# The last layer norm of a decoder trunk: the mean of the second half of the tokens from row sums of the weights

## The chip, the cores and the metric

The kernel runs on one core of one Trainium2 chip, as one launch. The metric is the device time in microseconds (us) of one execution. The kernel before took 795.58 us, the median of 3 runs (795.56 to 795.65).

## The reference, cut to what matters

256 tokens of width 2048 pass two layers (a pooling layer and a block-sparse attention layer, each with a memory branch). Only the end of the second layer is touched here: the output projection, the residual sum and the layer norm, all in fp32.

```
y = mixed @ w_out[i]                                  # (256, 2048) @ (2048, 2048)
h = layer_norm(DEEPNORM_ALPHA * h + y, ln_g[i], ln_b[i])

def layer_norm(x, g, b):
    mu = x.mean(-1, keepdims=True)
    var = jnp.square(x - mu).mean(-1, keepdims=True)
    return (x - mu) * lax.rsqrt(var + LN_EPS) * g + b
```

The output is this last h. Its norm needs, for each token, a mean and a variance over all 2048 columns.

## The kernel before, in words

**Precision.** Every fp32 operand of a product is split into a high and a low part (`split`, L72 to L75: ScalarE copies the high part, VectorE subtracts to get the low one), and each product is made of three matmuls: high by high, high by low, low by high.

**Blocks.** Weights come in blocks of 1024 columns a partition (512 KB). The list `items` holds them in the order in which TensorE uses them, and `run` (L174 to L212) walks it: loads are issued on SyncE (SP) some items ahead, each block is split (`prep`) three items ahead, and TensorE's matmuls of an item take 12 instructions. A block lands in one of four `raw` buffers, and its load waits until the split of the block four before has read that buffer; some blocks land in `ebuf`, `p` or `gate` instead (`SPOT`, L839). Each engine takes its instructions in the order in which the code writes them.

**The last projection.** `out_proj(1, range(3))` gives 24 items for the columns 0 to 1535. Its eight blocks for the last 512 columns (`KEEP`, L838 to L852) are loaded and split on the way, but not multiplied: both parts stay in `kept`, two planes of 16 x 512 columns in the tile `xm`. After `run`, TensorE works from `kept` alone (`last`, L879 to L889): for each of the 16 row blocks k three matmuls, so 48 for one accumulator. The tokens are two halves of 128, t = 0 and t = 1.

**The end of the kernel before.** TensorE does t = 0 over all 512 columns, then t = 1 over columns 1536 to 1791, then t = 1 over 1792 to 2047 (this last accumulator is `end`; two matmuls by an identity, the `seed`, add the residual to it). While these run, VectorE makes the norm of t = 0 and prepares t = 1: a preliminary mean m0 of the first 1536 columns is subtracted, the result is multiplied by g and split once more (`times_g`, L916). When `end` is there, its statistics give the true mean and deviation; TensorE then adds, to each piece of t = 1, the preliminary product by the identity and a product of six rows ("factor products": the two numbers of each token, transposed, times rows of g and b that `load_gb_rows` and `split_rows` made earlier, L820 to L836). What comes out of PSUM is scaled by the reciprocal deviation by ScalarE and VectorE and stored (L987 to L1002).

Of the kernel before, what the change touches and what calls it, by code (L numbers as in the profile page):

```python
# [11 lines left out]
F32 = mybir.dt.float32  # L12
# [37 lines left out]
def trunk(ctx: ExitStack, tc: tile.TileContext, a: dict, out: bass.AP):  # L50
# [6 lines left out]


    KX = KT * 2 * T
    near = sb.tile([P, 96], F32, name="near")  # L60
    xm = sb.tile([P, 2 * KX], F32R, name="xm")
    xT, memT = kept = [xm[:, i * KX:(i + 1) * KX].rearrange("p (k t) -> p k t", k=KT) for i in range(2)]
    zT = sb.tile([P, KT, 2 * T], F32R, name="zT")
    res = U0 = U1 = S0 = S1 = ident = mask = psc = eps_t = stats = ebuf = gate = None

# [58 lines left out]
    def prep_piece(it, c0, c1):  # L124
        raw = it["raw"][:, c0:c1]
        kind, *to = it["dst"] or ("w",)
        if kind == "act":
            t, kb = to
            k0, k1 = 4 * kb + c0 // T, 4 * kb + c1 // T
            split(t[:, k0:k1, :T], t[:, k0:k1, T:], raw.rearrange("p (k t) -> p k t", t=T))  # L130
            return
        if "w" not in it:
            it["w"] = to or (sb.tile([P, BLK], F32R, name="wh", bufs=W_BUFS),
                             sb.tile([P, BLK], F32R, name="wl", bufs=W_BUFS))
        wh, wl = it["w"]
# [682 lines left out]
    gbt = {}

    def load_gb_rows():  # L820
        raw = heads_tile("qq").rearrange("p a b -> p (a b)")[:6]
        gbt["rows"] = heads_tile("kk").rearrange("p a b -> p (a b)")[:6]
        gbt["hi"] = val_tile().rearrange("p a b c -> p (a b c)")[:6]
        gbt["sel"] = sb.tile([6, 2], F32, name="sel")
        for nm, p0 in (("ln_g", 0), ("ln_b", 3)):
            nc.scalar.dma_start(gbt["sel"][p0:p0 + 3], a["sel"][:3])
            nc.scalar.dma_start(f(raw)[p0:p0 + 3], a[nm][1][None, :].to_broadcast([3, D]))
        for n in range(4):
            later(31 + n, lambda n=n: split_rows(f(raw)[:, n * 512:(n + 1) * 512], n))

    def split_rows(raw, n):
        hi, rows = (gbt[k][:, n * 512:(n + 1) * 512] for k in ("hi", "rows"))
        nc.scalar.activation(hi, raw, AF.Copy)
        nc.vector.tensor_scalar_mul(f(hi), f(hi), gbt["sel"][:, 0:1])
        nc.vector.scalar_tensor_tensor(rows, raw, gbt["sel"][:, 1:2], f(hi),
                                       op0=ALU.mult, op1=ALU.add)  # L836

    KEEP = (9, 11, 13, 15, 17, 19, 21, 23)  # L838
    SPOT = {2: 0, 3: 1, 4: 2, 5: 0, 6: 1, 7: 2}  # L839
# [2 lines left out]
             lambda: gate[:, :4].rearrange("p a t -> p (a t)"))  # L842
    for j, it in enumerate(out_proj(1, range(3))):
        items.append(it)
        if j == 0:
            after(load_gb_rows)
        if j in KEEP:
            kb = KEEP.index(j)
            w3 = [t[:, 2 * kb:2 * kb + 2].rearrange("p k n -> p (k n)") for t in kept]
            item(a["w_out"][1, 3, kb], BLK, None, ("keep", *w3))  # L850
            if kb in SPOT:
                items[-1].update(lead=5 if kb == 2 else FAR, spot=spots[SPOT[kb]])  # L852

# [36 lines left out]

    def add(t, c0, c1, o):
        r = res[:, t, 1536 + c0:1536 + c1]
        nc.vector.scalar_tensor_tensor(r, r, ALPHA, o, op0=ALU.mult, op1=ALU.add)
        nc.vector.bn_stats(stats[:, t, 3 + (c0 > 0)], r)

    def finish(t, *chunks):
        for n in chunks:
            norm_chunk(n, t, gb1[n])
            for c0 in (n * 512, n * 512 + 256):
                store(t, c0, c0 + 256)  # L900

    cc = sb.tile([P, 6], F32R, name="cc").rearrange("p (v c) -> p v c", v=2)
    m0 = sb.tile([P, 2], F32, name="m0")
    ds = sb.tile([P, 2], F32, name="ds")
# [5 lines left out]
    place_of = {1: (0, 0), 0: (0, 512), 2: (1, 0), 3: (1, 512)}  # L910

    def both(n, c0, c1):
        i, at = place_of[n]
        return [t[:, at + c0:at + c1] for t in parts[i]]

    def times_g(n, c0=0, c1=512):  # L916
        r = res[:, 1, n * 512 + c0:n * 512 + c1]
        nc.vector.scalar_tensor_tensor(r, r, m0[:, 0:1], gb1[n][0][:, c0:c1],
                                       op0=ALU.subtract, op1=ALU.mult)
        hi, lo = both(n, c0, c1)  # L920
        nc.scalar.activation(hi, r, AF.Copy)
        return lambda: nc.vector.tensor_sub(lo, r, f(hi))

    def store(t, c0, c1, src=None, by=None):
        (by or nc.sync).dma_start(out[t * P:(t + 1) * P, c0:c1], res[:, t, c0:c1] if src is None else src)

    o = last(0, 0, 512)
    nc.vector.bn_aggr(m0, stats[:, 1, :3].rearrange("p a b -> p (a b)"))
    r = res[:, 1, 1792:]
    seed = both(3, 256, 512)  # L930
    nc.scalar.activation(seed[0], r, AF.Copy, scale=ALPHA)
    for low in [times_g(1), times_g(2), times_g(0, 256, 512)]:
        low()
    nc.vector.scalar_tensor_tensor(seed[1], r, ALPHA, f(seed[0]), op0=ALU.mult, op1=ALU.subtract)
    add(0, 0, 512, o)
    norm_stats(0, 4)
    o = last(1, 0, 256)
    finish(0, 0, 1)
    add(1, 0, 256, o)
    low = times_g(3, 0, 256)  # L940
    finish(0, 2)
    low()
    finish(0, 3)
    end = last(1, 256, 512, seed)


    pieces = (1, 0, 256), (1, 256, 512), (2, 0, 512), (0, 256, 512), (3, 0, 256)
    ts = {at: ps.tile([P, 512], F32, name="acc", bufs=4)[:, :at[2] - at[1]] for at in pieces[2:]}
    ts[pieces[0]] = ps.tile([P, 512], F32, name="o")[:, :256]
    ts[pieces[1]] = ps.tile([P, 2, 512], F32, name="s2")[:, 0, :256]  # L950
    for at in pieces:
        hi, lo = both(*at)
        mm(ts[at], one, hi, True, False)
        mm(ts[at], one, lo, False, False)
    nc.vector.bn_stats(stats[:, 1, 4], end)  # L955


    mv = sb.tile([P, 2], F32, name="mv", bufs=2)
    nc.vector.bn_aggr(mv, stats[:, 1].rearrange("p a b -> p (a b)"))  # L959
    rs = sb.tile([P, 1], F32, name="rs", bufs=2)  # L960

    def centred(n, c0, c1, src=None):
        r = res[:, 1, n * 512 + c0:n * 512 + c1]
        nc.vector.scalar_tensor_tensor(r, r if src is None else src, mv[:, 0:1], gb1[n][0][:, c0:c1], op0=ALU.subtract, op1=ALU.mult)  # L964

    def scaled(n, c0, c1):
        r = res[:, 1, n * 512 + c0:n * 512 + c1]
        nc.vector.scalar_tensor_tensor(r, r, rs, gb1[n][1][:, c0:c1], op0=ALU.mult, op1=ALU.add)
        store(1, n * 512 + c0, n * 512 + c1)

    nc.scalar.activation(ds[:, 1:2], mv[:, 1:2], AF.Sqrt, bias=eps_t[:, 0:1])
    nc.vector.tensor_sub(ds[:, 0:1], m0[:, 0:1], mv[:, 0:1])
    nc.scalar.activation(cc[:, :, 0:3:2], ds[:, :, None].to_broadcast([P, 2, 2]), AF.Copy)
    centred(3, 256, 512, end)
    nc.vector.tensor_sub(cc[:, :, 1], ds, f(cc[:, :, 0]))  # L975
    pt = ps.tile([P, 512], F32, name="pt")[:6, :P]
    nc.tensor.transpose(pt, f(cc).rearrange("p v c -> p (v c)"), ident)  # L977
    cct = sb.tile([P, P], F32R, name="ident")[:6]
    nc.scalar.activation(cct, pt, AF.Copy)  # L979
    for n, c0, c1 in pieces:  # L980
        mm(ts[n, c0, c1], cct, gbt["rows"][:, n * 512 + c0:n * 512 + c1], False, True)
    nc.vector.reciprocal(rs, ds[:, 1:2])
    scaled(3, 256, 512)
    centred(0, 0, 256)
    scaled(0, 0, 256)
    e = ebuf.rearrange("p j c -> p (j c)")

    def emptied(n, c0, c1):
        nc.scalar.activation(e[:, (n - 1) * 512 + c0:(n - 1) * 512 + c1], ts[n, c0, c1], AF.Copy, scale=rs)  # L989

    def sent(n, c0, c1, by):
        store(1, n * 512 + c0, n * 512 + c1, e[:, (n - 1) * 512 + c0:(n - 1) * 512 + c1], by)

    for at in pieces[:3]:
        emptied(*at)
    sent(*pieces[0], nc.sync)
    sent(*pieces[1], nc.scalar)
    for n, c0, c1 in pieces[3:]:
        r = res[:, 1, n * 512 + c0:n * 512 + c1]
        nc.vector.tensor_scalar_mul(r, ts[n, c0, c1], rs)  # L1000
        store(1, n * 512 + c0, n * 512 + c1)
    sent(*pieces[2], nc.scalar)  # L1002
# [55 lines left out]
```

## Time and profile before

| | |
|---|---|
| median of the runs | 795.58 us |
| the profiled execution | 795.69 us |
| its span, first to last instruction | 793.9 us |
| TensorE's granted clock, mean of the span | 0.997 |
| share of the chain that ended last | TensorE 98% |
| from the last product of `end` (785.86) to the end of the span | 8.0 us |

In the profile PE is TensorE, PEld its weight loads, DVE is VectorE, ACT is ScalarE, SP is SyncE; SPq and ACTq are the two queues on which DMAs are issued. Times are us from the start of the span; L70 is line 70 of the kernel. A row of the timeline gives start, busy time, engine, line, operation, out<-in, shapes and count, and in brackets how long the engine sat idle before it and for whom. Rows of grouped instructions give the busy time of all, the mean of one in ns, and the idle time before them.

### The profile page before, as it was taken

The page shows a single profiled execution, that of the slowest core. Times are in us where ns is not written, and L with a number is a line of the kernel's source. Part 1 is how long each engine was busy: PE and PEld are TensorE (multiplying, and loading weights), DVE is VectorE, ACT ScalarE, POOL GpSimd, SP SyncE. Part 2 cuts the span into 40 slices and gives each one's busy share as a digit, 9 for nine tenths or more (in the row PEclk, how much of TensorE's full clock was granted, in tenths as well). Part 3 has the DMA queues.
Part 4 walks back from the last instruction along what each step waited for, and adds up shares of the span by engine and source line. Part 5 has one row for each costly group of instructions (what it writes and reads, how often), then busy time and mean ns, then how long its engine had stood idle before and what let it go on. Part 6 is the DMA issues. An engine that isn't in the chain of part 4 may idle for free.

```text
span 793.9 us, 10030 instructions
## 1 busy us (share of the span) xinstructions
PE 787.4 (99%) x3664; PEld 657.3 (83%) x3664; DVE 574.3 (72%) x778; ACT 483.6 (61%) x595; POOL 0.2 (0%) x4
## 2 busy tenths in 40 slices
PE   9999999999999999999999999999999999999997
PEld 6888888888888888888888888888888888888886
DVE  6764588867488665668658786996578856878966
ACT  5666657576666543489865866566756566565531
POOL 0000000000000000000000000000000000000000
PEclk9999999999999999999999999999999999999998
DMA  9977566787768865599885685558764677747923
GB/s 338 404 239 168 188 187 185 214 243 213 216 233 214 293 206 190 188 287 264 247 239 160 193 229 194 179 174 223 240 185 163 196 214 226 210 163 260 332 70 106
DMA packets 121769, 172.16 MB, mean 217 GB/s; under 512 B 58226, under 2 KB 61042, under 8 KB 121458
## 3 DMA queue, kind: packets, MB, share of 16 engines
q1 hardware_dynamic: 119968, 167.41, 69.4%
q10 hardware_dynamic: 1752, 4.12, 1.5%
q8 instruction: 28, 0.46, 0.2%
q14 instruction: 21, 0.17, 0.1%
HBM read 156.29 MB, written 2.10 MB: 200 GB/s over the span
## 4 chain that ended last, share of the span: by engine, by line
PE 98%; DMA 1%; ACT 0%; DVE 0%; ACTq 0%; issue 0%
PE acc L70 91%; PE s L70 3%; PE o L70 3%; PE pt L70 2%; DMA raw<-in_w_mk 1%; ACT ebuf L989 0%; ACTq L113 0%; DVE stats L955 0%; DVE wh L159 0%; ACT L180 0%; DVE res L964 0%; DVE mv L959 0%; PE pt L977 0%; ACT ident L979 0%; DVE cc L975 0%
## 5 line engine op out<-in xcount | busy, mean ns | idle before, releaser
L75 DVE TENSOR_TENSOR wl<-raw,wh 128x1024 fp32r<-128x1024 f32 x234 | 279.3, 1206 | 137.7 <-ACT wh L74 133.7
L70 PE MATMUL acc<-wh,xm 128*128 128x512 f32 x1408 | 352.0, 390 | 0.2 <-DVE wh L159 0.2
L74 ACT ACTIVATE wh<-raw 128x1024 fp32r<-128x1024 f32 x234 | 239.1, 1041 | 139.3 <-PE acc L70 72.7
L70 PEld LDWEIGHTS acc<-wh,xm 128*128 128x128 f32 x1408 | 263.1, 188 | 54.4 <-ACT wh L158 0.6
L70 PE MATMUL acc<-wl,xm 128*128 128x512 f32 x704 | 191.7, 389 | 0.0
L70 PEld LDWEIGHTS acc<-wl,xm 128*128 128x128 f32 x704 | 132.2, 188 | 27.4
L70 PE MATMUL acc<-wh,zT 128*128 128x512 f32 x448 | 112.0, 390 | 0.0
L70 PEld LDWEIGHTS acc<-wh,zT 128*128 128x128 f32 x448 | 83.7, 188 | 17.1
L70 PE MATMUL acc<-xm 128*128 128x512 f32 x288 | 66.3, 389 | 0.0
L391 DVE STREAM_TRANSPOSE p<-ebuf 32x192 f32<-32x192 f32 (+1 forms) x160 | 63.3, 396 | 2.4
L70 PEld LDWEIGHTS acc<-xm 128*128 128x128 f32 x288 | 53.7, 188 | 10.9
L70 PE MATMUL acc<-wl,zT 128*128 128x512 f32 x224 | 61.0, 389 | 0.0
L70 PEld LDWEIGHTS acc<-wl,zT 128*128 128x128 f32 x224 | 42.1, 188 | 8.7
L75 DVE TENSOR_TENSOR xm<-raw,xm 128x1024 fp32r<-128x1024 f32 (+2 forms) x31 | 36.2, 1180 | 10.2 <-ACT xm L74 10.0
L74 ACT ACTIVATE xm<-raw 128x1024 fp32r<-128x1024 f32 (+2 forms) x31 | 30.5, 1015 | 6.1 <-PE acc L70 3.0
L290 ACT ACTIVATE pl<-acc 128x1024 uint16<-128x1024 uint16 x26 | 26.2, 1025 | 8.0 <-PE acc L70 8.0
L74 ACT ACTIVATE pp<-p 128x384 fp32r<-128x384 f32 (+1 forms) x20 | 11.2, 559 | 32.3 <-DVE p L391 32.3
L74 ACT ACTIVATE zT<-zf 128x512 fp32r<-128x512 f32 (+1 forms) x18 | 10.5, 584 | 21.6 <-DVE zf L397 17.0
L70 PE MATMUL acc<-xm,zT 128*128 128x256 f32 (+1 forms) x144 | 22.7, 318 | 0.0
L70 PEld LDWEIGHTS acc<-xm,zT 128*128 128x128 f32 x144 | 20.7, 190 | 1.9
L301 ACT ACTIVATE zf<-acc 128x512 f32<-128x512 f32 x16 | 9.5, 597 | 17.3 <-PE acc L70 17.2
L75 DVE TENSOR_TENSOR wl<-res,wh 128x1024 fp32r<-128x1024 f32 x12 | 14.6, 1224 | 6.2 <-ACT wh L74 5.9
(163 smaller groups left out, 532.4 us busy)
## 6 DMA issues: line engine op xcount, KB each, us to landing
raw<-in_w_in SPq DMA_DIRECT2D x123, 512.0 KB, 4.7
raw<-in_w_out SPq DMA_DIRECT2D x58, 512.0 KB, 4.2
raw<-in_w_sk SPq DMA_DIRECT2D x24, 512.0 KB, 4.3
raw<-in_w_sv SPq DMA_DIRECT2D x24, 512.0 KB, 3.6
raw<-in_w_mv SPq DMA_DIRECT2D x13, 512.0 KB, 5.5
raw<-in_w_mk SPq DMA_DIRECT2D x10, 512.0 KB, 4.9
res<-in_w_mk SPq DMA_DIRECT2D x5, 512.0 KB, 7.5
res<-in_w_in SPq DMA_DIRECT2D x5, 512.0 KB, 6.7
```

The lines of the kernel that those rows point to most:

```text
L70: nc.tensor.matmul(o, l, r, start=start, stop=stop, **kw)
L74: nc.scalar.activation(hi, src, AF.Copy)
L75: nc.vector.tensor_sub(lo, src, f(hi))
L290: nc.scalar.activation(pls[0][:, t], src.bitcast(U16).rearrange("p (n h) -> p h n", h=2), AF.Copy)
L301: nc.scalar.activation(src, acc, AF.Tanh, scale=0.5)
L391: nc.vector.transpose(self.p[32 * g:32 * g + 32, h * self.n:(h + 1) * self.n], self.e[32 * h:32 * h + 32, g * self.n:(g + 1) * self.n])
```

## The change

1. The planes of `kept` become 514 columns wide (`KW`). The two new columns of each row block hold the sum of that weight row over columns 1536 to 1791: while such a block is split (`prep_piece`, the new kind "rows"), a `tensor_reduce` of its raw columns writes two sums into `wsum`. After `run` the 16 sums are split into high and low and copied into the planes.
2. The order of the last three products becomes: t = 0 over 512 columns, t = 1 over columns 1792 to 2047 and the sum columns (258 wide), t = 1 over columns 1536 to 1791 with the seed (`end`). The sum column of the second product is the row sum of the third, so the mean of t = 1 is known before `end` is.
3. With this mean VectorE subtracts and multiplies by g all of t = 1 but `end`. When `end` is there, ScalarE squares it around the mean and sums (`accum_out`), takes the root with the variance of the rest as bias, and VectorE follows with `end`'s own subtraction, the reciprocal, and one operation a column (times the reciprocal deviation, plus b), whose six pieces are stored in turn from SP and ScalarE.
4. The factor rows, the second split, the identity products of the pieces, the transpose and the factor products are gone, and with them four small DMAs on ScalarE's queue. The norm of t = 0 is the same work in another order, stored in five DMAs instead of eight.

```diff
+    KW = 514
+    kept = [xm[:, i * KT * KW:(i + 1) * KT * KW].rearrange("p (k c) -> p k c", k=KT) for i in range(2)]
...
+        if kind == "rows":
+            k0, = to
+            raw = raw.rearrange("p (k c) -> p k c", k=2)
+            split(*(w[:, k0:k0 + 2, :512] for w in kept), raw)
+            nc.vector.tensor_reduce(wsum[:, k0:k0 + 2], raw[:, :, :256], op=ALU.add, axis=AX.X)
...
-            item(a["w_out"][1, 3, kb], BLK, None, ("keep", *w3))
+            item(a["w_out"][1, 3, kb], BLK, None, ("rows", 2 * kb))
...
+    sums = wsum[:, :, None].to_broadcast([P, KT, 2])
+    nc.scalar.activation(kept[0][:, :, 512:], sums, AF.Copy)
+    nc.vector.tensor_sub(kept[1][:, :, 512:], sums, f(kept[0][:, :, 512:]))
...
+    o = last(1, 256, KW)
...
+    nc.vector.scalar_tensor_tensor(low, o[:, 256:257], 1 / D, low, op0=ALU.mult, op1=ALU.add)
...
+    for n in range(3):
+        centred(1, n * 512, (n + 1) * 512, mu)
+    centred(1, 1792, 2048, mu)
+    end = last(1, 0, 256, seed)
+    nc.scalar.activation(ebuf[:, 0, :256], end, AF.Square, bias=nm, accum_out=total)
+    centred(1, 1536, 1792, mu, end)
+    nc.scalar.activation(sg, total, AF.Sqrt, bias=var, scale=1 / D)
+    nc.vector.reciprocal(rs, sg)
+    scaled(1, 0, 256, rs, nc.sync)
+    scaled(1, 256, 512, rs, nc.scalar)
+    scaled(1, 512, 1024, rs, nc.sync)
+    scaled(1, 1024, 1536, rs, nc.scalar)
+    scaled(1, 1536, 1792, rs, nc.sync)
+    scaled(1, 1792, 2048, rs, nc.scalar)
```

How it moves the instructions is seen at two places. The first is VectorE in the last projection, at the third and fourth of the eight kept blocks (landed in `ebuf` and `p`); a row is line, operation, out<-in and what it waits for. Before:

```order
L75 TENSOR_TENSOR xm_64<-ebuf_198,xm_64 128x1024 [waits DMAHW1_49,Activation_49]
L75 TENSOR_TENSOR wl_6005<-raw_6000,wh_6004 128x1024 [waits DMAHW2_49,PE_49,Activation_49]
L75 TENSOR_TENSOR wl_6023<-raw_6008,wh_6022 128x1024 [waits DMAHW4_49,PE_49,Activation_49]
L518 SCALAR_TENSOR_TENSOR res_1011<-res_1011,acc_5718 128x512 [waits PE_49]
L518 SCALAR_TENSOR_TENSOR res_1011<-res_1011,acc_5719 128x512 [waits PE_49]
L75 TENSOR_TENSOR xm_64<-p_6002,xm_64 128x1024 [waits DMAHW3_49,Activation_49]
L520 BN_STATS stats_197<-res_1011 128x6 [waits DVE_49]
```

The same place of the same engine after the change (the names carry other numbers, the line numbers by three or nine):

```order
L78 TENSOR_TENSOR xm_64<-ebuf_199,xm_64 128x2x512 [waits DMAHW5_49,Activation_49]
L139 TENSOR_REDUCE wsum_66<-ebuf_199 128x2
L78 TENSOR_TENSOR wl_6001<-raw_5996,wh_6000 128x1024 [waits DMAHW6_49,PE_49,Activation_49]
L78 TENSOR_TENSOR wl_6019<-raw_6004,wh_6018 128x1024 [waits DMAHW0_49,PE_49,Activation_49]
L527 SCALAR_TENSOR_TENSOR res_1012<-res_1012,acc_5719 128x512 [waits PE_49]
L527 SCALAR_TENSOR_TENSOR res_1012<-res_1012,acc_5720 128x512 [waits PE_49]
L78 TENSOR_TENSOR xm_64<-p_5998,xm_64 128x2x512 [waits DMAHW7_49,Activation_49]
L139 TENSOR_REDUCE wsum_66<-p_5998 128x2
```

Each kept block has a reduce directly behind its split, ahead of the low parts (`wl`) of the blocks that TensorE needs next; nothing else changed its place there.

The second place is VectorE from the preparation of t = 1 to its last instruction. Before, from the statistics of `end` on:

```order
L955 BN_STATS stats<-acc 128x6 [waits PE_49]
L959 BN_AGGR mv<-stats 128x2 [waits DVE_49]
L972 TENSOR_TENSOR ds<-m_6260,mv 128x1 [waits DVE_49]
L964 SCALAR_TENSOR_TENSOR res<-acc,mv,raw 128x256
L975 TENSOR_TENSOR cc<-ds,cc 128x2 [waits Activation_49]
L982 RECIPROCAL rs<-ds 128x1
L968 SCALAR_TENSOR_TENSOR res<-res,rs,raw 128x256 [waits DVE_49]
L964 SCALAR_TENSOR_TENSOR res<-res,mv,raw 128x256
L968 SCALAR_TENSOR_TENSOR res<-res,rs,raw 128x256 [waits DVE_49]
L1000 TENSOR_SCALAR res<-acc,rs 128x256 [waits PE_49] x2
```

The same engine after the change, from the last small operation on the variance (`eps_t` holds the single numbers of each token) on:

```order
L937 TENSOR_SCALAR eps_t<-eps_t 128x1 [waits DVE_49]
L890 SCALAR_TENSOR_TENSOR res<-res,eps_t,raw 128x512 x3
L890 SCALAR_TENSOR_TENSOR res<-res,eps_t,raw 128x256
L890 SCALAR_TENSOR_TENSOR res<-acc,eps_t,raw 128x256 [waits Activation_49]
L947 RECIPROCAL eps_t<-eps_t 128x1 [waits Activation_49]
L896 SCALAR_TENSOR_TENSOR res<-res,eps_t,raw 128x256 [waits DVE_49]
L896 SCALAR_TENSOR_TENSOR res<-res,eps_t,raw 128x256
L896 SCALAR_TENSOR_TENSOR res<-res,eps_t,raw 128x512 x2
L896 SCALAR_TENSOR_TENSOR res<-res,eps_t,raw 128x256 x2
```

All 2048 columns of t = 1 now pass VectorE behind the reciprocal, in six operations, where before it had two of 256 columns there (and one subtraction) and took two more pieces out of PSUM; ScalarE, which took three pieces out of PSUM, has none to take out.

More of the change, by code (lines that the diff above doesn't have):

```diff
@@ L59, in trunk @@
     KX = KT * 2 * T
-    near = sb.tile([P, 96], F32, name="near")
-    xm = sb.tile([P, 2 * KX], F32R, name="xm")
-    xT, memT = kept = [xm[:, i * KX:(i + 1) * KX].rearrange("p (k t) -> p k t", k=KT) for i in range(2)]
+    KW = 514
+    pad = 2 * KT * (KW - 2 * T)
+    near = sb.tile([P, 96 - pad], F32, name="near")
+    xm = sb.tile([P, pad + 2 * KX], F32R, name="xm")
+    xT, memT = (xm[:, pad + i * KX:pad + (i + 1) * KX].rearrange("p (k t) -> p k t", k=KT) for i in range(2))
+    kept = [xm[:, i * KT * KW:(i + 1) * KT * KW].rearrange("p (k c) -> p k c", k=KT) for i in range(2)]
     zT = sb.tile([P, KT, 2 * T], F32R, name="zT")
@@ L130, in prep_piece @@
             split(t[:, k0:k1, :T], t[:, k0:k1, T:], raw.rearrange("p (k t) -> p k t", t=T))
+            return
+        if kind == "rows":
[3 more added lines that the diff above has]
+            nc.vector.tensor_reduce(wsum[:, k0:k0 + 2], raw[:, :, :256], op=ALU.add, axis=AX.X)
             return
@@ L815, in trunk @@
         proj_n(xT, [a["w_sv"][grp, kb] for kb in range(8)], to_values(v, 0), place=in_mem)
[L818 to L836, printed above, removed]
+    wsum = sb.tile([P, KT], F32, name="wsum")
     KEEP = (9, 11, 13, 15, 17, 19, 21, 23)
@@ L844, in trunk @@
         items.append(it)
-        if j == 0:
-            after(load_gb_rows)
         if j in KEEP:
             kb = KEEP.index(j)
-            w3 = [t[:, 2 * kb:2 * kb + 2].rearrange("p k n -> p (k n)") for t in kept]
-            item(a["w_out"][1, 3, kb], BLK, None, ("keep", *w3))
+            item(a["w_out"][1, 3, kb], BLK, None, ("rows", 2 * kb))
             if kb in SPOT:
@@ L892, in add @@
         r = res[:, t, 1536 + c0:1536 + c1]
[L893 to L904, printed above, removed]
@@ L907, in trunk, with store, centred @@
-    parts = [[sb.tile([P, BLK], F32R, name=nm, bufs=W_BUFS) for nm in ("wh", "wl")] for _ in range(2)]
+        nc.vector.scalar_tensor_tensor(r, r, ALPHA, o[:, :c1 - c0], op0=ALU.mult, op1=ALU.add)
+        nc.vector.bn_stats(stats[:, t, 3], r)
+    def store(t, c0, c1, by=None):
+        (by or nc.sync).dma_start(out[t * P:(t + 1) * P, c0:c1], res[:, t, c0:c1])
+    def centred(t, c0, c1, mean, src=None):
+        r = res[:, t, c0:c1]
+        n, at = c0 // 512, c0 % 512
+        nc.vector.scalar_tensor_tensor(r, r if src is None else src, mean, gb1[n][0][:, at:at + c1 - c0],
+                                       op0=ALU.subtract, op1=ALU.mult)
@@ L908, in trunk, with scaled @@
+    def scaled(t, c0, c1, rs, by=None):
+        r = res[:, t, c0:c1]
+        n, at = c0 // 512, c0 % 512
+        nc.vector.scalar_tensor_tensor(r, r, rs, gb1[n][1][:, at:at + c1 - c0], op0=ALU.mult, op1=ALU.add)
+        store(t, c0, c1, by)
     one = sb.tile([P, BLK], F32R, name="wh", bufs=W_BUFS)[:, :P]
+    seed = [sb.tile([P, BLK], F32R, name=nm, bufs=W_BUFS)[:, :256] for nm in ("wh", "wl")]
+    m0 = eps_t[:, 4:6]
+    mu, nm, low, total, off, sg, rs, var = (eps_t[:, 4 * i + 8:4 * i + 9] for i in range(8))
@@ L909, in trunk @@
     nc.scalar.activation(one, ident, AF.Copy)
[L910 to L922, printed above, removed]
@@ L924, in store @@
-    def store(t, c0, c1, src=None, by=None):
-        (by or nc.sync).dma_start(out[t * P:(t + 1) * P, c0:c1], res[:, t, c0:c1] if src is None else src)
+    sums = wsum[:, :, None].to_broadcast([P, KT, 2])
+    nc.scalar.activation(kept[0][:, :, 512:], sums, AF.Copy)
+    nc.vector.tensor_sub(kept[1][:, :, 512:], sums, f(kept[0][:, :, 512:]))
     o = last(0, 0, 512)
-    nc.vector.bn_aggr(m0, stats[:, 1, :3].rearrange("p a b -> p (a b)"))
-    r = res[:, 1, 1792:]
-    seed = both(3, 256, 512)
+    r = res[:, 1, 1536:1792]
@@ L931, in trunk @@
     nc.scalar.activation(seed[0], r, AF.Copy, scale=ALPHA)
-    for low in [times_g(1), times_g(2), times_g(0, 256, 512)]:
-        low()
     nc.vector.scalar_tensor_tensor(seed[1], r, ALPHA, f(seed[0]), op0=ALU.mult, op1=ALU.subtract)
+    nc.vector.tensor_reduce(low, r, op=ALU.add, axis=AX.X)
+    nc.vector.tensor_scalar_mul(low, low, ALPHA / D)
     add(0, 0, 512, o)
     norm_stats(0, 4)
[L937 to L1002, printed above, removed]
+    o = last(1, 256, KW)
+    mv, rs0 = lnst[0]
+    for c0, c1, step in ((0, 512, 1), (512, 1024, 1), (0, 256, 2), (256, 512, 2), (512, 1024, 2),
+                         (1024, 1536, 1), (1536, 2048, 1)):
+        if step == 1:
+            centred(0, c0, c1, mv[:, 0:1])
+        else:
+            scaled(0, c0, c1, rs0)
@@ new lines, in trunk @@
+    add(1, 256, 512, o)
+    scaled(0, 1024, 1536, rs0)
+    nc.vector.bn_aggr(m0, stats[:, 1, :4].rearrange("p a b -> p (a b)"))
+    part = 1792 / D
+    nc.vector.scalar_tensor_tensor(low, o[:, 256:257], 1 / D, low, op0=ALU.mult, op1=ALU.add)
+    scaled(0, 1536, 2048, rs0)
+    nc.vector.scalar_tensor_tensor(mu, m0[:, :1], part, low, op0=ALU.mult, op1=ALU.add)
+    nc.vector.tensor_sub(off, m0[:, :1], mu)
+    nc.vector.tensor_scalar_mul(nm, mu, -1.0)
+    nc.vector.scalar_tensor_tensor(var, off, off, m0[:, 1:2], op0=ALU.mult, op1=ALU.add)
@@ new lines, in trunk @@
+    nc.vector.tensor_scalar(var, var, part, EPS, op0=ALU.mult, op1=ALU.add)
+    for n in range(3):
[8 more added lines that the diff above has]
+    scaled(1, 256, 512, rs, nc.scalar)
```

## The prediction

> **What bounds the kernel now.** I read the page first: its span, its engines and the chain that ended last.
>
> ```profile
> span 793.9 us, 10030 instructions
> PE 787.4 (99%) x3664; PEld 657.3 (83%) x3664; DVE 574.3 (72%) x778; ACT 483.6 (61%) x595; POOL 0.2 (0%) x4
> PE 98%; DMA 1%; ACT 0%; DVE 0%; ACTq 0%; issue 0%
> ```
>
> TensorE is the chain for 98% of the span and is busy for 99% of it. So the change can act in two ways only: it can alter what follows TensorE's last product, or it can make TensorE wait where it doesn't now. For the first I read the chain in order of time over the last 50 us, and the stores.
>
> ```profile
> 739.87 45.99 PE acc L70 x249
> 785.88 0.44 DVE stats L955
> ...
> 788.51 1.42 ACT ebuf L989 x3
> ...
> 789.38 0.95 ACTq L925 DMA_DIRECT2D out<-ebuf  x2
> 789.84 0.91 SPq L925 DMA_DIRECT2D out<-res  x2
> ...
> out<-res SPq DMA_DIRECT2D x12, 128.0 KB, 1.9
> out<-ebuf ACTq DMA_DIRECT2D x1, 256.0 KB, 2.8
> ```
>
> TensorE's last product of `end` is over at 739.87 + 45.99 = 785.86; the last scaling by ScalarE ends at 788.51 + 1.42 = 789.93. The second store of ScalarE's queue (256 KB) starts at about 789.95 and lands 2.8 later, at 792.75; SP's last (128 KB) starts at about 790.37 and, with 1.9 to 2.2, lands by 792.6. The span ends 1.15 after the later of the two. So of the 8.0 us behind TensorE 4.1 are the chain to the last store issue and 3.9 the store and the end. All that the change can win lies in the 4.1.
>
> For the second way I read the stretches of the last projection and, in them, VectorE's and TensorE's timelines.
>
> ```profile
> 735.00:740.00 5.00, 5.00 (x24) 4.14 (x23) 5.00 (x7) 2.50 (x4) 0.00 (x0) 1.00 1.01 393
> 745.00:750.00 5.00, 5.00 (x24) 4.14 (x23) 5.00 (x6) 2.91 (x3) 0.00 (x0) 1.00 0.93 312
> ```
>
> After the stretch and its length come TensorE's busy time, its weight loads', VectorE's, ScalarE's and GpSimd's, the clock, the DMA share and GB/s. In both stretches VectorE has no free time at all (5.00 of 5.00) and the DMA engines hardly any, and just there the change gives VectorE more to do. This is the place at which it could do harm.
>
> **The reduces in the last projection.** Eight `tensor_reduce` of 2 x 256 columns come behind the splits of the kept blocks. The trace has the operation in the shape 128x512 to 128x2, and its neighbours on both sides.
>
> ```profile
> L362 DVE TENSOR_REDUCE nb<-p 128x2 f32<-128x256 f32 x6 | 2.5, 420 | 0.2
> L362 DVE TENSOR_REDUCE nb<-p 128x2 f32<-128x512 f32 x6 | 4.1, 676 | 0.0
> L362 DVE TENSOR_REDUCE nb<-s 128x4 f32<-128x1024 f32 x4 | 4.9, 1220 | 5.3 <-PE s L70 5.3
> ```
>
> I take 0.68, from the row with the same element count; the bounds are 0.42 and 1.22, if the gap between the two runs of 256 columns costs as much as reading across it. Whether TensorE feels them is a matter of lead: how long before its use a low part (`wl`) is ready.
>
> ```profile
> 725.51 0.43 DVE L497 TENSOR_TENSOR s<-s,zf 128x256 f32<-128x256 f32 x1 [1.95 <-ACT zf L496]
> 728.32 1.23 DVE L75 TENSOR_TENSOR xm<-raw,xm 128x1024 fp32r<-128x1024 f32 x1 [0.26 <-ACT xm L74]
> 734.33 1.22 DVE L75 TENSOR_TENSOR wl<-raw,wh 128x1024 fp32r<-128x1024 f32 x1 [0.24 <-ACT wh L74]
> 744.19 1.21 DVE L75 TENSOR_TENSOR wl<-raw,wh 128x1024 fp32r<-128x1024 f32 x1
> 748.18 2.35 DVE L75 TENSOR_TENSOR wl<-raw,wh 128x1024 fp32r<-128x1024 f32 x2
> 752.26 1.23 DVE L75 TENSOR_TENSOR wl<-raw,wh 128x1024 fp32r<-128x1024 f32 x1 [0.60 <-ACT wh L74]
> 754.73 1.23 DVE L75 TENSOR_TENSOR wl<-raw,wh 128x1024 fp32r<-128x1024 f32 x1 [1.24 <-ACT wh L74]
> ...
> 748.54 1.07 PE L70 MATMUL acc<-wl,zT 128*128 128x512 f32 x4
> 753.99 1.07 PE L70 MATMUL acc<-wl,zT 128*128 128x512 f32 x4
> ```
>
> The first kept block's reduce falls ahead of the 1.95 us that VectorE waits before 725.51, and is paid there. The second's is at 728.32. From it to the `wl` of 744.19 VectorE waits only once more, 0.24, and meets four reduces: 4 x 0.68 - 0.24 = 2.48 late. That `wl` ends at 745.40 and is first read at 748.54, so its lead of 3.14 shrinks to 0.66. This is the tightest place. At 748.18 five reduces have passed, 3.16; that `wl` would end at 752.5 and is read at 753.99. Behind it the idle 0.60 and 1.24 take back 1.84, and after 757 VectorE has nothing but adds. By this TensorE never waits: cost nothing, and the cover is 0.66 us of lead.
>
> The loads hang on VectorE too: a `raw` buffer comes free when its split is done.
>
> ```profile
> 729.57 1.46 SPq L113 DMA_DIRECT2D raw<-in_w_out  x2
> 736.65 1.06 ACT L74 ACTIVATE wh<-raw 128x1024 fp32r<-128x1024 f32 x1 [1.40 <-DMA raw<-in_w_out]
> 740.73 1.04 ACT L74 ACTIVATE wh<-raw 128x1024 fp32r<-128x1024 f32 x1
> ```
>
> SP's load at 729.57 leaves 0.02 after the split of 728.32 ends (729.55), so it will leave 0.68 later, and those behind it on SP's queue, later by at most what VectorE is late by. ScalarE's high part for the `wl` of 744.19 is written at 740.73: even 2.5 late it is there before VectorE comes for it at 746.7. So the loads add nothing to VectorE's own delay. The DMAs issue later, but no more bytes move, and four small ones of ScalarE's queue are gone. What left VectorE and ScalarE here (the factor rows) lay beside TensorE's products and wins nothing.
>
> **TensorE's last three products.** The middle one is 258 wide in 48 matmuls. From rows of eight and twelve, 512 columns take (1.98 - 0.39) / 7 = 0.227 and 256 take (1.60 - 0.28) / 11 = 0.120, so a column is 0.42 ns and 48 x 2 of them 0.04 us. The two sum columns are written behind VectorE's last statistics of the projection, which end at 764.66. The middle product comes after 48 matmuls of 512 columns that themselves come behind the projection (48 x 0.227 = 10.9 us before it): no wait. TensorE ends at 785.90.
>
> ```profile
> 744.01 1.98 PE L70 MATMUL acc<-wh,zT 128*128 128x512 f32 x8
> 784.24 1.60 PE L70 MATMUL acc<-xm,zT 128*128 128x256 f32 x12
> 763.97 0.69 DVE L522 BATCH_NORM_STATS2 stats<-res 128x6 f32<-128x512 f32 x1
> ```
>
> **VectorE up to the end of TensorE.** Everything that `end` doesn't need is now queued on VectorE ahead of it. I replay it from the rows of the norm of t = 0.
>
> ```profile
> 769.51 1.81 DVE L918 SCALAR_TENSOR_TENSOR res<-res,m,raw 128x512 f32<-128x512 f32 x3
> 776.29 0.73 DVE L548 SCALAR_TENSOR_TENSOR res<-res,mv,raw 128x512 f32<-128x512 f32 x1
> 777.05 0.75 DVE L549 SCALAR_TENSOR_TENSOR res<-res,rs,raw 128x512 f32<-128x512 f32 x1
> 777.72 0.74 DVE L548 SCALAR_TENSOR_TENSOR res<-res,mv,raw 128x512 f32<-128x512 f32 x1
> 787.51 0.48 DVE L968 SCALAR_TENSOR_TENSOR res<-res,rs,raw 128x256 f32<-128x256 f32 x1
> 787.91 0.48 DVE L964 SCALAR_TENSOR_TENSOR res<-res,mv,raw 128x256 f32<-128x256 f32 x1
> L982 DVE RECIPROCAL rs<-ds 128x1 f32<-128x1 f32 x1 | 0.2, 157 | 0.0
> ```
>
> An operation that needs nothing of the one before it starts 0.67 behind one of 512 columns (777.05 to 777.72) and 0.40 behind one of 256 (787.51 to 787.91). Start is 776.29, as before. Five of 512 and two of 256 take 4.15, to 780.44; sum and statistics of the middle product about 0.8 (two of 256), two more of 512 about 1.35, seven small ones at an estimated 0.10 to 0.20 (0.157 in the row of the reciprocal) together about 1.0 (783.6); then three of 512 and one of 256 of t = 1, 2.4: free at about 786.0. VectorE and TensorE finish together; VectorE is 0.1 behind and costs nothing, since ScalarE's square comes first.
>
> The Trainium skill ("VectorE: DVE Perf Modes", section "The DRAIN you can't avoid") says that the next operation doesn't start until the pipe is empty, so that only fewer operations help, though it adds that one that isn't held starts earlier. By its main sentence each would cost its whole duration, VectorE would be free 1.1 later, and the sum below would be 796.3. The trace speaks for the addition: three operations of 748, 748 and 480 ns took 1.81 together, not 1.98.
>
> **Behind TensorE.** The pieces are these.
>
> ```profile
> L367 ACT ACTIVATE ebuf<-s,nb 128x256 f32<-128x256 f32 x16 | 7.4, 476 | 1.5 <-DVE nb L363 1.5
> L367 ACT ACTIVATION_READ_ACCUMULATOR ebuf<-s,nb 128x1 f32 x16 | 3.3, 207 | 0.0
> L971 ACT ACTIVATE ds<-mv,eps_t 128x1 f32<-128x1 f32 x1 | 0.3, 294 | 4.9 <-DVE mv L959 4.9
> ```
>
> The square of 256 columns out of PSUM with its sum is 0.48 + 0.21: 785.92 to 786.61. VectorE's subtraction on `end` waits for ScalarE in the new order, so it runs 786.63 to 787.11 beside the root (0.29, done at 786.92); the reciprocal 0.16 brings 787.25. Six operations start 0.40, 0.40, 0.67, 0.67 and 0.40 apart: the last starts at 789.79 and ends at 790.27. Each store leaves behind its operation, in turn on two queues, so the last (128 KB, ScalarE's queue) leaves at 790.30. Before, the last one left at 790.37: four steps over TensorE and three scalings by ScalarE are gone, but VectorE alone now does all 2048 columns behind the root, 2.54 + 0.48 us. What is won is the landing: 128 KB for 256 KB, 2.0 for 2.8. With 1.9 to 2.8 as bounds it lands at 792.3 (792.2 to 793.1), and with 1.15 behind it the span is 793.45. That is 0.45 less than 793.9; 795.69 - 0.45 = 795.24. The profiled execution is 0.11 above the median of 795.58, so by the median it would be 795.13; between the two I take **795.2**.
>
> **Rivals.** A difference of 0.2% is 1.6 us; less than that a measurement of this kernel can hardly be told from no change.
>
> *VectorE pays whole durations.* Each operation from 776 on costs its full length: free at 787.1, subtraction to 787.8, reciprocal to 788.0, then 3.4 more: last store at 791.4, 796.3. Against it stand the rows above. Still no change by 0.2%.
>
> *The reduces reach TensorE.* The place is the `wl` of 744.19. With R for one reduce, it is 4R - 0.24 late with 3.14 of lead: TensorE waits from R = 0.85 on. At 1.22, the upper row, it waits 1.5 and the time is 796.7; if each of the two runs of 256 cost as much as the 0.68 row, 1.36, it waits 2.1 and the time is 797.3, slower by over 0.2% (from R = 1.34 on). For it speaks that VectorE and the DMA engines are full just there; against it that the reduce rows follow the element count (420, 676, 1220) over gaps as well.
>
> *The change does nothing for the end.* If the subtraction and the root overlap less, or the last landing is 2.8 because two queues store at once, the 0.45 is lost: 795.7.
>
> A gain over 1.6 us would need the last store to leave before 789; six operations of VectorE behind the root don't allow it.
>
> **How the numbers follow.** The forecast 795.2 has 0.62, "nothing won" 0.2, whole durations 0.09, TensorE held up 0.07 (nearly all of it counted as slower), and 0.02 stays for a gain that the trace doesn't show. The first three lie within 0.2%: 0.91. The range runs from 794.7 (from the unrounded 795.13: shortest landing 0.1, no wait of the subtraction 0.1, the read of the sum beside the square 0.2) to 796.3 (whole durations), and leaves out TensorE's wait.
>
> **What would show it.** Right: no idle time of PE before 786; `tensor_reduce` rows of 0.68; VectorE's `wl` rows between 735 and 752 up to 3 us later; the square at 785.9, the reciprocal at 787.1, the last store at 790.3. Wrong: reduces above 0.85; PE waiting for `wl` near 748.5; VectorE still on t = 1 after 786.5 when the square is done; a wait of TensorE at the 258-wide product; or a last landing later than 792.8.

## The result and the profile after

The changed kernel takes **801.02 us** (801.00 to 801.31, 6 runs) and the kernel before, on the same chip, 795.63 us (795.56 to 795.73, 6 runs): a ratio of 1.0069, with a 95% interval of 1.0059 to 1.0079. The forecast was 795.2 and "no change", with a range of 794.7 to 796.3; the changed kernel is 5.4 us slower and lies outside it.

The first lines of the page after:

```profile
span 799.5 us, 9976 instructions
PE 791.2 (99%) x3648; PEld 655.6 (82%) x3648; DVE 573.3 (72%) x781; ACT 477.9 (60%) x585; POOL 0.2 (0%) x4
PE 99%; DVE 0%; issue 0%; DVEq 0%; ACT 0%
```

TensorE is busy for 791.2 us where it was 787.4, with 16 instructions fewer. A wait doesn't add to its busy time: in experiment 12, where it does wait, it is busy for 785.3 us, as in experiment 1, where it doesn't. All that it waits for in the whole program is one line of the waits. TensorE is 5.7 us later here than in the kernel before (730.75 for 725.06, below), so the place that the prediction called the tightest, 744 to 749, now lies between 750 and 755. Neither that stretch nor the one ahead of it has a wait (columns as in the prediction's fence of the same view):

```profile
PE s L73 <- PEq L1001: 0.8, 1, 0.8
```

```profile
745.00:750.00 5.00, 5.00 (x23) 4.10 (x23) 5.00 (x8) 3.27 (x4) 0.00 (x0) 1.00 0.90 336
750.00:755.00 5.00, 5.00 (x24) 4.09 (x23) 5.00 (x7) 3.11 (x4) 0.00 (x0) 1.00 0.74 262
```

The groups kept apart by shape show where the time is: count, busy us of all, then the mean ns of one, in which neighbours overlap. Before:

```profile
L70 PE MATMUL acc<-wh,xm 128*128 128x512 f32 x1408 | 352.0, 390 | 0.2 <-DVE wh L159 0.2
L70 PE MATMUL acc<-wl,xm 128*128 128x512 f32 x704 | 191.7, 389 | 0.0
L70 PE MATMUL acc<-wh,zT 128*128 128x512 f32 x448 | 112.0, 390 | 0.0
L70 PE MATMUL acc<-wl,zT 128*128 128x512 f32 x224 | 61.0, 389 | 0.0
```

After:

```profile
L73 PE MATMUL acc<-wh,xm 128*128 128x512 f32 x1408 | 354.5, 391 | 0.0
L73 PE MATMUL acc<-wl,xm 128*128 128x512 f32 x704 | 193.7, 392 | 0.0
L73 PE MATMUL acc<-wh,zT 128*128 128x512 f32 x448 | 112.8, 391 | 0.0
L73 PE MATMUL acc<-wl,zT 128*128 128x512 f32 x224 | 61.6, 392 | 0.0
```

Nothing was added to these 2784 matmuls, and their operands and order are those of before; yet they take a little longer, in all 2.5 + 2.0 + 0.8 + 0.6 = 5.9 us. The chain in order of time says from when on. Before (start, length, and how many in a row):

```profile
46.81 43.52 PE acc L70 x192
...
269.75 144.19 PE acc L70 x636
...
725.06 60.81 PE acc L70 x314
```

After:

```profile
47.41 43.95 PE acc L73 x192
...
271.68 145.57 PE acc L73 x636
...
730.75 61.34 PE acc L73 x314
```

At 47 us, long before the first `tensor_reduce` of the change (725.6) and on code that the diff doesn't touch, 192 products already take 0.43 more; 636 take 1.38 more, which is 2.2 ns each. TensorE's last product ends at 730.75 + 61.34 = 792.09, against 785.87: 6.22 later. Behind it the changed kernel is the quicker one: 799.5 - 792.09 = 7.41 against 793.9 - 785.87 = 8.03, so 0.6 us shorter, where the forecast had about 0.5.

What distinguishes the products is in none of the change's operations but in a line of the changed kernel that the shortened diff leaves out and the prediction passed over: `wsum = sb.tile([P, KT], F32, name="wsum")` (L827), a new tile of 64 bytes in each partition. It is allocated behind `zT`, so all that is allocated later, `res`, `raw`, `wh` and `wl`, moves up by 64 bytes. These are the start addresses in the built programs (bytes within a partition). No trace shows them; their distances follow from the order and the sizes of the tiles in the two kernels:

```
          near   xT     zT     wsum   res    raw     wh      wl
before    1152   1536   67072  -      99840  116224  132608  148992
after     1152   1536   67072  99840  99904  116288  132672  149056
```

The change takes care of the room that the 514 columns need: it cuts `near`, which no instruction uses, from 96 to 32 columns (128 bytes), so that `xT` and `zT` stay. It doesn't do so for `wsum`. Before, `wh`, `wl`, `xT` and `zT` lie whole multiples of 4096 bytes from each other; after, `wh` and `wl` lie 64 bytes off that. A product takes two operands: a block of 128 x 128 that TensorE loads and holds (from `xm`, of which `xT` is a part, or from `zT`), and 512 columns that it streams past it (from `wh` or `wl`).

### The profile page after: what moved, and what is told of

Read it like the earlier page. It is cut to its first block, busy times and chain, and to the rows that moved or that the text cites. A ratio compares the mean times of both kernels' runs of the same rounds, so it can differ in the third digit from the quotient of the medians.

```text
span 799.5 us, 9976 instructions
## 1 busy us (share of the span) xinstructions
PE 791.2 (99%) x3648; PEld 655.6 (82%) x3648; DVE 573.3 (72%) x781; ACT 477.9 (60%) x585; POOL 0.2 (0%) x4
## 4 chain that ended last, share of the span: by engine, by line
PE 99%; DVE 0%; issue 0%; DVEq 0%; ACT 0%
PE acc L73 91%; PE s L73 4%; PE o L73 3%; PE pt L73 2%; DVE res L896 0%; DVE res L890 0%; DVEq L1005 0%; ACT ebuf L944 0%; DVE eps_t L947 0%
## 5 line engine op out<-in xcount | busy, mean ns | idle before, releaser
L73 PE MATMUL acc<-wl,xm 128*128 128x512 f32 x704 | 193.7, 392 | 0.0
L73 PE MATMUL acc<-xm,zT 128*128 128x512 f32 (+2 forms) x144 | 22.9, 319 | 0.0
```

Of the source, the lines that this page charges most:

```text
L73: nc.tensor.matmul(o, l, r, start=start, stop=stop, **kw)
```

## The experiments

Each time is compared with that of the kernel before on the same chip. In the expectations theory A holds the place of the tiles responsible, and rival B the new work (VectorE's reduces, the wider planes). The later theories A1, P, C and G and their rivals are narrower questions about the place, each told in its expectation.

**1. The sums without the tile.** The changed kernel, with the 16 sums put into the unused `near`:

```diff
-    wsum = sb.tile([P, KT], F32, name="wsum")
+    wsum = near[:, :KT]
```

> The changed kernel with one line altered: the 16 sums live in the unused tile in front of the weights planes instead of in a new 64-byte tile behind them, so that every later tile has the start address that it has in the kernel before. Theory A (the 64 bytes shift the weight tiles off a multiple of 128 bytes, and each 512-wide product pays about 2 ns for it): 12 products take 2.72 again instead of 2.75, and the time falls by 5.5 to 6.0, to 795.0 to 795.5. Rival B (the reduces and the later loads slow TensorE, or anything else in the new work): stays at 801.0 within 0.5.

Measured: 795.21 us (795.12 to 795.49), ratio 0.9994 [0.9984, 1.0003]. All of the change's work is in it, at the old addresses, and the loss is gone. The chain's long row of this kernel:

```profile
269.77 144.19 PE acc L73 x636
```

Its length is that of before to the hundredth. So the new work costs nothing that can be measured, and the tile's place costs 5.8 us (801.02 - 795.21).

**2 to 4. The place without the work.** The kernel before with an unused tile ahead of `res`, of 64, 128 and 32 bytes:

```diff
+    shift = sb.tile([P, 16], F32, name="shift")
     scr = sb.tile([P, 4 * BLK], F32, name="res")
```

(with 32 and 8 columns for the other two).

> The kernel before with an unused tile of 64 bytes a partition in front of the tiles that follow the planes, and nothing else. Theory A: every 512-wide product with a shifted weight tile slows by about 2 ns, 12 of them take 2.75, the time is 801.0 to 801.8. Rival B: 795.6 within 0.3.

> The kernel before with an unused tile of 128 bytes at that place. If what counts is a multiple of 128 bytes (or of 64 with another cause), the time is 795.6 within 0.3. If a multiple of 256 or 512 bytes counts (the weight tiles now start at 128 past one), it is near 801. Rival B: 795.6.

> The kernel before with an unused tile of 32 bytes at that place, the smallest step of the tiles' addresses. Theory A with any grain of 64 bytes or more: near 801, or more if the cost grows with the distance from a multiple. Rival B, or a grain of 32 bytes: 795.6.

Measured: 801.71 us, ratio 1.0075 [1.0060, 1.0091], with 64 bytes; 812.48, 1.0211 [1.0195, 1.0226], with 128; 814.13, 1.0232 [1.0217, 1.0247], with 32. The long row of the chain with 64, 128 and 32 bytes:

```profile
271.66 145.57 PE acc L70 x636
```

```profile
275.29 147.78 PE acc L70 x636
```

```profile
276.17 148.38 PE acc L70 x636
```

The first is the loss of the changed kernel, without one instruction of the change. The other two went otherwise than expected: 128 bytes had been thought harmless or as harmful as 64, and more than 801 with 32 bytes only if the cost grows with the distance. The loss is 2.2 ns a product with 64, 5.6 with 128 and 6.6 with 32: it doesn't grow with the step.

**5. Everything moved.** `near` grows by 64 bytes, so that all tiles move together:

```diff
-    near = sb.tile([P, 96], F32, name="near")
+    near = sb.tile([P, 112], F32, name="near")
```

> The kernel before with its unused tile in front of everything 64 bytes longer, so that planes, split activations and weights all start 64 bytes later and keep their distances. Theory A1 (the start address of the operand that streams counts by itself): as in the run with 64 bytes behind the planes, 801.7, or up to 0.7 more since the 288 products with weights kept in the planes are shifted too. Rival A2 (what counts is the distance between the streamed weights and the operand held in the array, or another tile): 795.7.

Measured: 795.79 us, ratio 1.0002 [0.9993, 1.0012]. `wh` and `wl` start at the same addresses as in the changed kernel, and their products run as before:

```profile
L70 PE MATMUL acc<-wh,xm 128*128 128x512 f32 x1408 | 352.1, 390 | 0.0
```

So it isn't where a tile starts that counts; it is how far tiles lie from each other.

**6. Only what lies behind the weights.** 32 unused bytes ahead of `ident`:

```diff
+        shift = sb.tile([P, 8], F32, name="shift")
         ident = sb.tile([P, P], F32, name="ident")
```

> The kernel before with 32 unused bytes behind the weight tiles: only the tiles after them (identity, gates, queries, keys, values, statistics) start 32 bytes later. Theory A: the weight tiles stand where they stood, so 795.7 to 796.0. If the slow-down of the run with 32 bytes came from any of the later tiles: up to 814.

Measured: 796.00 us, ratio 1.0005 [0.9995, 1.0014]. The tiles behind `wl` have no part in it.

**7. Only the weights.** 32 bytes between `raw` and `wh`, so that `res` and `raw` stay:

```diff
+        shift = sb.tile([P, 8], F32, name="shift")
         wh, wl = block["w"] = [sb.tile([P, BLK], F32R, name=nm, bufs=W_BUFS) for nm in ("wh", "wl")]
```

> The kernel before with an unused tile of 32 bytes between the raw tiles and the wh and wl tiles: res and raw stay where they were, wh and wl move together. Theory P (the distance between what TensorE streams, wh and wl, and what it holds, the planes and zT, decides): the same as with 32 bytes ahead of res, 813.5 to 814.7. Rival (the distance of the raw or res tiles from the planes decides, so loads or the splits that read them collide with something): 795.6 to 796.0. Rival 2 (the distance of raw from wh decides): neither, some other loss.

Measured: 814.15 us, ratio 1.0234 [1.0217, 1.0251], as with `res` and `raw` moved as well (4), and so is the long row:

```profile
276.14 148.38 PE acc L70 x636
```

Together with 5 and 6 this leaves one pair: what TensorE streams (`wh`, `wl`) and what it holds (`xm`, `zT`). Where the loads land, in `raw`, has no part in it.

**8. Only the low parts.** 32 bytes between `wh` and `wl`:

```diff
-        wh, wl = block["w"] = [sb.tile([P, BLK], F32R, name=nm, bufs=W_BUFS) for nm in ("wh", "wl")]
+        wh = sb.tile([P, BLK], F32R, name="wh", bufs=W_BUFS)
+        shift = sb.tile([P, 8], F32, name="shift")
+        wl = sb.tile([P, BLK], F32R, name="wl", bufs=W_BUFS)
+        block["w"] = [wh, wl]
```

> The kernel before with the 32 unused bytes between the high and the low parts of the weights: the high parts keep their addresses, the low parts and all behind them are shifted. Theory A: only the products with a low part pay, a third of all (960 of 512 columns at 6.4 ns each, 6.1 us): 801.5 to 802.2, and rows of products with a high part stay at 389 ns. A cause outside TensorE's streamed operand: 795.7 or 814.

Measured: 809.98 us, ratio 1.0181 [1.0164, 1.0198]: a miss of 8 us.

```profile
L70 PE MATMUL acc<-wh,xm 128*128 128x512 f32 x1408 | 357.4, 393 | 0.0
L70 PE MATMUL acc<-wl,xm 128*128 128x512 f32 x704 | 196.8, 396 | 0.0
```

The low parts are slow, as expected, but so are the high parts, though neither `wh` nor what is held with it has moved. The two next experiments ask why.

**9. The same without the splits.** From the ninth block on ScalarE and VectorE split only 8 columns, and TensorE multiplies what the buffers hold:

```diff
+        thin = len(held) >= 2 * W_BUFS and not to
...
+            it["w"] = to or (held[-W_BUFS] if thin else
...
+        if thin:
+            split(wh[:, c0:c0 + 8], wl[:, c0:c0 + 8], raw[:, :8])
+            return
```

> The kernel with 32 bytes between the wh and the wl tiles, and with the splitting of the weights left out behind the first eight blocks: ScalarE and VectorE split only 8 columns of each block, TensorE multiplies what the buffers still hold (so the output is of other weights), with the same addresses, products and order as before. Theory P (TensorE's own two reads collide, and a slow product puts the next one out of step): high-part products stay at about 231 ns apart and low-part ones at 234, 807 to 811 in all. Rival (the writes of the shifted wl by VectorE, or the reads of raw, take turns from TensorE's reads): high-part products go back to 227 ns, the low-part ones too if it is all of it; 795 to 797, or 800 to 802 if only the high-part ones go back.

Measured: 809.88 us, ratio 1.0179 [1.0164, 1.0194]. The page and the groups:

```profile
PE 801.0 (99%) x3664; PEld 657.3 (81%) x3664; DVE 334.7 (41%) x778; ACT 289.4 (36%) x595; POOL 0.2 (0%) x4
...
L70 PE MATMUL acc<-wh,xm 128*128 128x512 f32 x1408 | 357.5, 393 | 0.0
...
L70 PE MATMUL acc<-wl,xm 128*128 128x512 f32 x704 | 196.8, 396 | 0.0
```

VectorE and ScalarE are busy 41% and 36% of the span, where in the kernel before it was 72% and 61%, and both groups of products are as in 8. The splits' reads of `raw` and writes of `wh` and `wl` don't cause it.

**10. The same without a stream from the shifted tile.** The low-part products stream `wh` a second time; `wl` is still written, 32 bytes off:

```diff
-                h, l = (moving(w, wblk[kb]) for w in (wh, wl))
+                h, l = (moving(w, wblk[kb]) for w in (wh, wh))
```

> The kernel with 32 bytes between the wh and the wl tiles, where the four low-part products of each block stream the block's high parts a second time (so the output lacks the low parts of the weights); number, order and sizes of the products are unchanged, and ScalarE and VectorE split as before. No product of the body then streams from a shifted tile. Theory C (a product that streams from a shifted tile puts the following ones out of step, so that products at unchanged addresses are slow too): all products 226 or 227 ns apart, 795.4 to 796.2. Rival (the shifted wl slows the high-part products by itself, by its being written or by where it lies): high-part products stay at about 231 ns, 803 to 810.

Measured: 796.30 us, ratio 1.0008 [0.9997, 1.0019], 0.1 above the expected range and far below the rival's.

```profile
L70 PE MATMUL acc<-wh,xm 128*128 128x512 f32 x2112 | 484.7, 390 | 0.2 <-DVE wh L162 0.2
```

This group now has the low-part products too (2112 = 1408 + 704), and all are at 390 ns again. So a product that streams from a shifted tile makes others slow that don't. The starts of single matmuls in the traces show the same. Here is the mean time (ns) from the start of each of a block's twelve products to the next start, over some 103 blocks of each kernel: h1 to h8 are the eight high parts, l1 to l4 the four low ones, and the number in brackets is that of the experiment.

```
                  h1    h2    h3    h4    h5    h6    h7    h8    l1    l2    l3    l4
before           226.5 226.9 226.6 226.6 226.9 226.6 226.6 226.9 226.6 226.6 226.9 226.6
after            226.6 229.3 230.8 226.5 229.3 230.8 226.5 229.3 230.9 226.6 229.3 230.8
32 B, all (4)    231.6 234.7 232.6 234.6 231.5 234.7 232.6 234.3 231.9 234.7 232.4 234.5
32 B, wl (8)     240.5 224.5 230.8 235.7 228.3 232.4 230.7 226.6 235.9 230.9 235.8 234.1
32 B, wl (9)     240.7 224.3 230.8 235.7 228.4 232.4 230.7 226.6 236.0 230.8 235.8 234.1
```

The losses have a fixed pattern. It comes in turns of three after the change, and it is the same to 0.2 ns in 8 and in 9, though the other engines do quite different work there.

**11. A step that may be free.** In experiment 1 the `kept` products give finer steps: their rows are 2056 bytes apart (514 columns of 4 bytes), so each of the 16 lies 8 bytes further off a multiple of 256, and the second plane another 128. The first 12 of the 48 products of 512 columns, ns from one start to the next, with experiment 1 above and the changed kernel below:

```
e1     227 234 226 236 234 233 233 230 226 236 234 238
after  229 231 234 230 239 233 233 230 225 237 234 238
```

In experiment 1 the first and third stream the one row that lies a multiple of 256 bytes (257 x 256) from `zT`: 227 and 226. The others of the 48 spread from 225 to 238, so this is a hint and no more: a step of 256 bytes may be free.

The two lines also show how far a slow product reaches. These products and what they hold lie at the same addresses in both kernels; only the products ahead of them stream from a shifted tile in the changed kernel. There the first five differ from experiment 1 (229 for 227, 234 for 226); from the sixth on the two lines agree to 1 ns.

The test of the hint is the changed kernel with a larger `wsum`, of which 16 columns are used:

```diff
-    wsum = sb.tile([P, KT], F32, name="wsum")
+    wsum = sb.tile([P, 64], F32, name="wsum")[:, :KT]
```

> The changed kernel with one number changed: wsum takes 256 bytes a partition in place of 64 (16 of its 64 columns are used), so that res, raw, wh and wl lie 256 bytes further from the planes than in the kernel before, instead of 64. Theory G (a step of 256 bytes is free: in the kernel with the sums in near, the 48 kept 512-wide products begin 227 and 226 ns apart where the streamed row lies a multiple of 256 bytes from the stationary blocks, and 225 to 238 apart elsewhere): 795.0 to 795.6, twelve products 2.72 us. Rival 1 (only the very distances of the kernel before are free, or multiples of 512): 801 to 814, as with 32, 64 and 128 bytes.

Measured: 795.15 us, ratio 0.9994 [0.9985, 1.0003].

```profile
269.64 144.19 PE acc L73 x636
```

The tile costs nothing when it is four times as large. Written so, the change makes no difference to the time that can be measured, which is what was forecast.

**12. The cover of the reduces.** In the kernel of experiment 1 each reduce is done twice:

```diff
+            nc.vector.tensor_reduce(near[:, KT + k0:KT + k0 + 2], raw[:, :, :256], op=ALU.add, axis=AX.X)
             nc.vector.tensor_reduce(wsum[:, k0:k0 + 2], raw[:, :, :256], op=ALU.add, axis=AX.X)
```

> The changed kernel with its sums in the front tile, and each of the eight reduces done twice. The replay of the prediction: the low part that ended 2.1 late with single reduces ends 2.4 later still and 1.3 behind TensorE's need; TensorE waits about 1.3 near 748.5 and the time is 796.3 to 796.8. If the cover is larger than the replay says: 795.2. If the later loads add to it: 797.5 or more.

Measured: 796.65 us, ratio 1.0014 [1.0004, 1.0023], 1.44 us over experiment 1. The waits of TensorE in its last projection and the stretch that holds the wait:

```profile
PE acc L73 <- DVE wl L78: 1.2, 1, 1.2
```

```profile
745.00:750.00 5.00, 3.75 (x18) 2.79 (x16) 5.00 (x8) 3.54 (x4) 0.00 (x0) 1.00 0.68 261
```

TensorE waits once, 1.2 us, for a `wl`, between 745 and 750. That is the place that the prediction worked out from rows, and its lead of 3.14 us fits: by the rows of experiment 1 (below) the `wl` comes 2.07 late with single reduces, each further one costs 0.59, and 2.07 + 4 x 0.59 - 3.14 = 1.29.

## Why the prediction was wrong

**The step that failed** is the first: "So the change can act in two ways only: it can alter what follows TensorE's last product, or it can make TensorE wait where it doesn't now." There was a third way: each product can itself take longer. The sum took the 2784 products of the body as unchanged (0.227 us from start to start) and never asked what a new tile does to them. By the rows of the groups this adds 5.9 us, nearly all of the 6.22 by which TensorE ends later; PE's busy time says the same, 791.2 for 785.3 in experiment 1. None of the rivals had it either, and the list of signs looked for idle time of PE, while the sign was PE's busy time.

The Trainium skill ("SBUF — State Buffer", section "Who interferes with whom") gives TensorE two read ports of SBUF, one for the streamed operand and one for weight loads, and calls them independent. Where the distances are multiples of 256 bytes the rows agree: a load of 188 ns (PEld) lies beside every product and the products follow at 227 ns. At 32, 64 and 128 bytes off the products follow later, and there the measurement decides. The loads don't grow: here is one group before and, below it, in experiment 4 with 32 bytes, where a product takes 6.6 ns more. That it is the two ports that collide isn't shown.

```profile
L70 PEld LDWEIGHTS acc<-wh,xm 128*128 128x128 f32 x1408 | 263.1, 188 | 54.4 <-ACT wh L158 0.6
```

```profile
L70 PEld LDWEIGHTS acc<-wh,xm 128*128 128x128 f32 x1408 | 262.6, 187 | 63.1 <-ACT wh L158 0.2
```

**The other steps held.** They can be read in experiment 1, where the products have their old length; its time, 795.21, is that of the forecast, 795.2. Its VectorE in the last projection:

```profile
728.35 1.23 DVE L78 TENSOR_TENSOR xm<-raw,xm 128x1024 fp32r<-128x1024 f32 x1 [0.26 <-ACT xm L77]
729.50 0.68 DVE L139 TENSOR_REDUCE near<-raw 128x2 f32<-128x512 f32 x1
730.09 2.35 DVE L78 TENSOR_TENSOR wl<-raw,wh 128x1024 fp32r<-128x1024 f32 x2
...
745.07 0.68 DVE L139 TENSOR_REDUCE near<-gate 128x2 f32<-128x512 f32 x1
...
746.26 1.21 DVE L78 TENSOR_TENSOR wl<-raw,wh 128x1024 fp32r<-128x1024 f32 x1
```

- *The reduces*: 0.68 each, as taken. The next operation starts 0.59 behind one (729.50 to 730.09), so the `wl` of 744.19 is 746.26 - 744.19 = 2.07 late where 2.48 was said, and its lead shrinks to 1.07, not to 0.66. TensorE doesn't wait; experiment 12 shows that it does at twice the work. The rival "The reduces reach TensorE" falls.
- *TensorE's last three products*: the term was too small. TensorE ended at 785.90 by the forecast and ends at 725.08 + 60.99 = 786.07. By the groups below, the 258-wide product is not it (5.9 us, as the 256-wide one); the 48 matmuls of 512 columns take 11.3, and in the kernel before 11.0 (389 ns). Their rows of 514 columns lie off the multiples of 256 bytes. It looks like the same effect, at 5 ns each; VectorE stands still for 8.8 us there, waiting for TensorE, so it isn't VectorE that disturbs. No run tests this place alone.

```profile
L73 PE MATMUL acc<-xm,zT 128*128 128x512 f32 x48 | 11.3, 394 | 0.0
L73 PE MATMUL acc<-xm,zT 128*128 128x258 f32 x48 | 5.9, 282 | 0.0
L73 PE MATMUL acc<-xm,zT 128*128 128x256 f32 x48 | 5.9, 281 | 0.0
```

- *VectorE's replay and the end*: the lines from there to the last operation.

```profile
783.68 2.46 DVE L890 SCALAR_TENSOR_TENSOR res<-res,eps_t,raw 128x512 f32<-128x512 f32 x4
...
786.10 0.47 ACT L944 ACTIVATE ebuf<-acc,eps_t 128x256 f32<-128x256 f32 x1 [9.65 <-PE acc L73]
786.47 0.19 ACT L944 ACTIVATION_READ_ACCUMULATOR ebuf<-acc,eps_t 128x1 f32 x1
...
786.70 0.48 DVE L890 SCALAR_TENSOR_TENSOR res<-acc,eps_t,raw 128x256 f32<-128x256 f32 x1 [0.56 <-ACT ebuf L944]
787.10 0.15 DVE L947 RECIPROCAL eps_t<-eps_t 128x1 f32<-128x1 f32 x1
787.29 3.00 DVE L896 SCALAR_TENSOR_TENSOR res<-res,eps_t,raw 128x256 f32<-128x256 f32 x6
```

VectorE is free at 783.68 + 2.46 = 786.14 (forecast 786.0) and waits for the square. The subtraction starts at 786.70 (786.63), the reciprocal ends at 787.25 (787.25), the last operation at 790.29 (790.27); the span is 793.5 (793.45). The read of the sum starts 0.10 before the square's row ends, which gives back 0.1 of TensorE's later end. "VectorE pays whole durations" falls with the six operations in 3.00, for which it had 3.4. (One of that rival's steps doesn't add up: 787.1 and a subtraction of 0.48 make 787.6, not 787.8, so the rival, and the top of the range with it, should have been 796.1, not 796.3.) "The change does nothing for the end" falls too, as far as one profile each can tell: 7.4 us behind TensorE for 8.0. In the times the gain of about 0.5 us stays within the interval (0.9984 to 1.0003).

**What stays open.** Shown is that the distance between the tiles that TensorE streams and those that it holds sets the rate, and that the splits of VectorE and ScalarE and the place where the loads land have no part in it. Not shown is what collides inside: that it is the weight load of the next product beside the running stream fits all runs, but no run separates the two reads. Nor is it known why 64 bytes cost a third of what 32 cost, or by what the loss passes on to products at unmoved addresses. Steps of 32, 64, 128 and 256 bytes were tried for the whole body, 8-byte ones only in the 48 `kept` products.

## What to carry to other kernels

Where one engine is busy for 99% of the span, a new tile is a change to every instruction of that engine that uses a tile behind it: compare the tiles' addresses before and after, and give a small tile 256 bytes (experiment 11), or put it behind the tiles that the products read (experiment 6). The sign is a row of the same group, same shape and count, that is about 1% longer, at the start of the program as at its end; no view of waits shows it. What counts is what lies between the tiles that a product reads: 64 bytes more ahead of all of them cost nothing (experiment 5).

## What was not expected of the hardware

- The rate of 512-wide products depends on the distance between streamed and held tiles: 226.7 ns from start to start at the multiples of 256 bytes that were run (experiments 1, 5 and 11); per product 2.2 ns more at 64 bytes off, 5.6 at 128, 6.6 at 32 (1.38, 3.59 and 4.19 us over 636 products). In the whole program that is 0.75%, 2.1% and 2.3%.
- Where the weights are read from, as such, doesn't matter: with all tiles 64 bytes further, 1.0002 [0.9993, 1.0012].
- A slow stream makes products slow that have not moved: with only `wl` off, high-part products go from 390 to 393 ns, in a fixed pattern between 224 and 241 from start to start, the same with and without the splits of VectorE and ScalarE beside them. In the one place where a trace shows the end of it, it is gone after five products (experiment 11).
- The 256-wide products of the last norm are not slowed: 48 of 258 columns take 5.9 us, as 48 of 256 do, with rows that lie just as far off as those of the slowed 512-wide ones; in the kernel before, 96 of 256 took 11.8.
